# Two edits to a hand-scheduled two-network kernel: other numbers in the emission scheduler's cost table, and the first tile's last normalization released earlier

## The chip, the cores and the metric

The kernel runs on one core of a Trainium2 chip (trn2). The metric is device time in microseconds (us) of one launch, the median of three runs; the profile shows one further execution of the same program. Engines carry the profile's names: PE is the matrix engine (PEld its weight loads), DVE the vector engine, ACT the scalar engine, POOL the third elementwise engine, SP the engine whose queue issues most DMAs.

## The reference, cut to what matters

Two networks of two layers each run one after the other on 256 tokens of width 1024, in float32.

```python
def first_block(x, c, ...):
    sc = jax.nn.silu(c)
    for i in range(DEPTH):
        mod = sc @ w_ada[i] + b_ada[i]
        sh_m, sc_m, g_m, sh_f, sc_f, g_f = jnp.split(mod, 6, axis=-1)
        h = modulate(x, norm_mix[i], sh_m, sc_m)
...
            y = moba_attention(h, w_qkv[j], w_o[j], q_gain[j], k_gain[j])
...
            y = short_conv(h, w_in[j], conv_w[j], w_out[j])
        x = x + g_m[:, None, :] * y
        h = modulate(x, norm_ffn[i], sh_f, sc_f)
        x = x + g_f[:, None, :] * swiglu(h, w_gate_up[i], w_down[i])
    return x
```

The second network has, in layer 2, a gated linear recurrence (`hgrn2_mix`) beside a small attention into 256 memory tokens, in layer 3 a stick-breaking attention beside the same kind of memory attention. After each of them comes `wo`, a layer norm with the residual (`post_norm`), then a mixture of 16 experts (two per token, chosen inside one of four groups) and a last layer norm, `(xf - mu) * rsqrt(var + eps) * g + b`, whose result is the output of the kernel.

## The kernel before, in words

The 256 tokens are two tiles of 128 rows, T0 and T1, which share every weight. Weights arrive as units of 128 x 1024 float32 (512 KB each, one DMA of the SP queue, tile `raw`, issued at L555 in `pump`). For float32 accuracy a dense unit is split into two parts: `hi`, a cast (L506 on ACT, or L502 on DVE), and `lo`, the remainder (a subtraction, L487, on DVE). A block is then three products, hi by hi, hi by lo and lo by hi, all issued at L452 in `mm`. Activations are transposed on PE against the identity `identr` (L464 in `tr`) and split in the same way. So a quarter of a dense product (`gemm`, q0 to q3) is six matmuls with 512 columns on PE, beside one cast and one subtraction of 1024 columns for its next weights.

`Body` holds one Python generator per piece of work: a program for each tile, one that prepares weights (`prep_task`), one for the modulation vectors (`ada_task`), one for the transposed and split inputs of a layer (`lhsT_task`), one for the experts. `Sched.run` steps them one at a time: it picks, among those whose conditions hold at a model time `sch.now`, the one with the highest priority. Every helper issues its instruction at once and then moves a model clock: `mm` and `tr` add to `sch.now`, helpers for ACT and DVE to `tA` and `tD`, `pump` adds to `dma_t` for each unit. On the chip the engines run their instructions in the order in which they were issued, and wait for real semaphores. The model numbers therefore choose an order; they appear nowhere else in the program.

In the feed-forward layers (`ffn`, eleven steps e0 to e10 per tile) a step is four quarters of gate and up, then `Silu` and a product on the gate (ACT L480, DVE L487), two transposes of the hidden tile `tH`, its split, and a down product of twelve matmuls. The next layer's input is made by `modnorm` (a sum of squares on ACT L478, a power on POOL L521, a scaling on DVE L492) and `lhsT_task` (eight transposes, four activations L484 and a cast L506 for each half, a subtraction L487). Between ffn1 and layer 2 there is no norm: T0's and T1's `x` are transposed directly.

The last layer norm is done in two ways. T1 goes through `affine_rows`: four instructions on DVE (L498) and a send after each half. T0 goes through `affine_pool`: a bias `nb` on DVE (L494), two activations on ACT (L484), then for the first half a multiplication and an addition on POOL (L1316), for the second half the same two on DVE (L487). Two events order them: `fin1` is set when T1's statistics have been issued, `sentf1` when T1's four DVE instructions have been. Behind it all, `go` copies a flag that says whether a second, denser version of the experts must run; it does not run on this data.

Of the kernel before, what the change touches and what calls it, by code (L numbers as in the profile page):

```python
# [72 lines left out]
def make_plan(again=False):  # L73
# [75 lines left out]
    for nm, kd in moe(0)[:16] + lnrows("m0") + moe(0)[16:]:  # L149
        put(nm, kd, 1)  # L150
# [4 lines left out]
    for nm, kd in moe(1)[:16] + lnrows("m1") + moe(1)[16:]:  # L155
        put(nm, kd, 1)
# [145 lines left out]
class Body:  # L302
# [148 lines left out]
    def mm(self, out, lhsT, rhs, start, stop, shared=False):  # L451
        self.nc.tensor.matmul(out, lhsT, rhs, start=start, stop=stop, skip_group_check=shared)  # L452
        n = 1
        for d in rhs.shape[1:]:
            n *= d
        m = out.shape[0]
        if lhsT.dtype == F32R:
            c = max(0.227 * n / 512, 0.108)
        else:
            c = max(0.86 * n / 512, 0.224 if m > 64 else 0.112) * (0.26 if m <= 32 and n == 512 else 0.52 if m <= 64 and n == 512 else 1.0)  # L460
        self.sch.now += c

    def tr(self, out, in_):
        self.nc.tensor.transpose(out, in_, self.ident)  # L464
        self.sch.now += 0.109

    def act(self, out, in_, func, bias=0.0, scale=1.0, accum_out=None):
        want = {AF.Exp: "natural_log_exp_and_others", AF.Ln: "natural_log_exp_and_others", AF.Silu: "silu_and_others"}.get(func)
# [68 lines left out]
    def pump(self):  # L537
        while self.can_dma():
            i = self.nextdma
            if i == 4 and not self.again:  # L540
                self.nc.sync.dma_start(self.x[0], self.x_d[0])
                self.dma_t += 1.46
                self.x0_t = self.dma_t + 2.0
            if i == 18 and not self.again:
                self.nc.sync.dma_start(self.x[1], self.x_d[1])
                self.nc.sync.dma_start(self.cst, self.consts_d[:, 128:])
                self.dma_t += 2.3
                self.x1_t = self.dma_t + 2.0
            if self.plan.kind[i] == "row":
                t = self.ring.tile([128, 1024], F32, tag="u", name="row")  # L550
                r = self.rows_d[self.where[self.plan.src[i]]]
                self.nc.sync.dma_start(t, bass.AP(tensor=r.tensor, offset=r.offset, ap=[[0, 128], [1, 1024]]))
            else:
                t = self.ring.tile([128, 1024], F32, tag="u", name="raw")
                self.nc.sync.dma_start(t, self.units_d[self.where[self.plan.src[i]]])  # L555
            self.tiles[i] = t
            self.dma_t = max(self.dma_t, self.sch.now) + 1.3
            self.arr[i] = self.dma_t + 2.0
            if self.plan.kind[i] != "dense":
                self.ready[i] = self.arr[i]  # L560
            self.raw_used += 1
            if self.plan.kind[i] == "dense":
                self.rawdense += 1
            self.nextdma += 1
# [335 lines left out]
    def mem_task(self):  # L900
# [43 lines left out]
        self.fS(4)  # L944

    def mem_attention(self, T, layer, qm, mm):

        hi, lo = [mm[:, i * 256:(i + 1) * 256].rearrange("p (k t) -> p k t", k=2) for i in range(2)]
# [355 lines left out]
    def affine_pool(self, T, nm, src):  # L1304

        x, sv = self.x[T], self.stat[T]
        rows = self.rows(nm)
        yield [self.unit(r) for r in rows]
        nb = self.tm(1)
        self.ts(nb, sv[:, 0:1], sv[:, 2:3], -1.0, ALU.mult, ALU.mult)  # L1310
        for b in range(2):
            c = slice(b * 512, (b + 1) * 512)
            self.act(x[:, c], src[b], AF.Identity, bias=nb, scale=sv[:, 2:3])
        ops = list(zip((ALU.mult, ALU.add), [self.tiles[r] for r in rows]))
        for op, r in ops:
            self.nc.gpsimd.tensor_tensor(x[:, :512], x[:, :512], r[:, :512], op)  # L1316
        self.nc.scalar.dma_start(self.out_d[T][:, :512], x[:, :512])
        yield f"sent{nm}"
        for op, r in ops:
            self.tt(x[:, 512:], x[:, 512:], r[:, 512:], op)  # L1320
        self.send(T, slice(512, 1024))
        for r in rows:
            self.done(r)
# [26 lines left out]
    def wo_postnorm(self, T, layer, mix, mm):  # L1350
        front = not (self.again or self.last[T])

        def res(b):
            def f(acc):
                self.residual_half(T, b, acc)
                if front:
                    self.sch.spawn(self.front_half(T, b, layer), 0)
            return f

        if T == 0:  # L1360
            self.LAG = 8
        tail = [(mm[:, j * 128:(j + 1) * 128], mm[:, 256 + j * 128:384 + j * 128]) for j in range(2)] + [f"memat{layer}_{T}"]
        yield from self.gemm(T, self.ids[f"wo{layer}"], mix, [res(0), res(1)], tail=tail)
        self.fS(2)
        self.fH()
        self.stats(T, self.bns[T])
        if not front:
            yield from self.affine_rows(T, f"m{layer}", self.halves(T))
# [24 lines left out]
    def layer2(self, T):  # L1393
# [71 lines left out]
        def b6(acc):  # L1465
            nonlocal mm
            qm, mm = self.tH(), self.tH(F32R)
            self.scopy(qm[:, :256], acc[:, :256])
            self.free()
            self.sch.spawn(self.mem_attention(T, 0, qm, mm), 0)  # L1470
# [664 lines left out]
    def moe(self, T, layer):  # L2135
        if T == 0:
            self.SMIN = SM0
            self.sel, self.selT, self.xs = {}, {}, {}
            self.sch.spawn(self.moe_task(layer), 2)
        yield from self.moe_front(T, layer)  # L2140
        st = self.tm(12)
        for b in range(2):
            yield f"moe{layer}_{T}_{b}"
            if T == 1 and not self.last[T]:
                yield lambda: self.tD - 0.3
            acc = self.out[T]
            self.nc.vector.bn_stats(st[:, 6 * b:6 * b + 6], acc[b])
            self.onD(512)
        self.stats(T, st)
        if T == 0 and self.last[T]:  # L2150
            yield f"fin{layer}"
            yield from self.affine_pool(T, f"f{layer}", acc)
        else:
            self.sch.set(f"fin{layer}")
            yield from self.affine_rows(T, f"f{layer}", acc)
            self.sch.set(f"sentf{layer}")
        self.free(2)
# [125 lines left out]
```

## Time and profile before

| | us |
|---|---|
| median of three runs | 1204.48 (1203.82, 1204.48, 1207.32) |
| the profiled execution, its own time | 1204.19 |
| its span, first to last instruction | 1202.4 |
| PE busy / idle inside the span | 1144.9 / 57.5 |
| DVE busy, ACT busy, POOL busy | 725.0, 549.1, 44.8 |
| mean granted clock of PE | 0.988 |

The time outside the span is 1.8 us. PE is busy for 95% of the span, so most of what a change of order can move is inside the 57.5 us in which PE stands still (7 us of them at the start, before the first weights have been prepared, and 13 us at the end, behind the last matmul). The list of waits says what PE waited for, the timeline where; the table of windows gives busy time, granted clock and DMA share for each stretch.

### The profile page before, as it was taken

How to read it: one execution, taken by the hardware profiler on the slowest of the kernel's cores; microseconds unless marked ns; L12 is line 12 of the kernel's file. 1: busy time of each engine (PE TensorE's matmuls, PEld its weight loads, DVE VectorE, ACT ScalarE, POOL GpSimd, SP SyncE). 2: the span in 40 equal slices, each digit the busy share in tenths (PEclk: the TensorE clock that was granted, in tenths of full speed). 3: DMA queues.
4: the chain of work that ended last, by engine and by line, in shares of the span. 5: the costliest groups of instructions: out<-in, count | busy, mean ns of one | idle time of the engine just before them, and what ended most of it. 6: DMA issues, size and time to landing. Idle time of an engine off the chain costs nothing. (4 is left out here: it accounts for less than half of the span.)

```text
span 1202.4 us, 16685 instructions
## 1 busy us (share of the span) xinstructions
PE 1144.9 (95%) x6344; PEld 823.7 (69%) x6344; DVE 725.0 (60%) x1121; ACT 549.1 (46%) x913; POOL 44.8 (4%) x65
## 2 busy tenths in 40 slices
PE   7999989999998999999999999999999899999995
PEld 4777768888886787788887789886333577673331
DVE  4577667667577987665556567678221766564214
ACT  4655465434446455544434484553121456631211
POOL 0021000000000000000000000100000100000001
PEclk9999999999999999999999999999999899999998
DMA  9976768777664866466556233377999842587994
GB/s 375 409 306 228 256 222 302 262 268 269 244 239 155 340 247 215 158 211 217 205 194 209 86 125 105 123 277 266 378 409 408 311 142 72 188 333 306 408 408 159
DMA packets 83544, 301.72 MB, mean 251 GB/s; under 512 B 9408, under 2 KB 9824, under 8 KB 83456
## 3 DMA queue, kind: packets, MB, share of 16 engines
q1 hardware_dynamic: 82224, 298.37, 67.1%
q0 software_dynamic: 944, 1.82, 0.6%
q8 instruction: 52, 0.85, 0.3%
q10 hardware_dynamic: 288, 0.38, 0.1%
q14 instruction: 36, 0.29, 0.1%
HBM read 298.83 MB, written 2.10 MB: 250 GB/s over the span
## 5 line engine op out<-in xcount | busy, mean ns | idle before, releaser
L452 PE MATMUL bk<-hi,tS 128*128 128x512 f32 (+1 forms) x1760 | 586.9, 399 | 13.7 <-ACT hi L506 8.0
L452 PEld LDWEIGHTS bk<-hi,tS 128*128 128x128 f32 x1760 | 332.6, 190 | 87.2 <-ACT hi L506 8.7
L487 DVE TENSOR_TENSOR lo<-raw,hi 128x1024 fp32r<-128x1024 f32 x266 | 317.1, 1221 | 67.4 <-ACT hi L506 65.7
L452 PE MATMUL bk<-lo,tS 128*128 128x512 f32 (+1 forms) x880 | 345.0, 392 | 1.6 <-DVE lo L487 1.6
L506 ACT CAST hi<-raw 128x1024 fp32r<-128x1024 f32 x263 | 265.0, 1049 | 20.8 <-DMA raw<-in_units_dram 8.2
L452 PEld LDWEIGHTS bk<-lo,tS 128*128 128x128 f32 x880 | 167.4, 190 | 35.0 <-DVE lo L487 3.4
L480 ACT ACTIVATE tH<-bk 128x256 f32<-128x256 f32 (+1 forms) x100 | 44.8, 449 | 253.8 <-PE bk L452 253.6
L452 PE MATMUL bk<-hi,tH 128*128 128x512 f32 x384 | 133.1, 397 | 1.4 <-ACT tH L506 1.4
L487 DVE TENSOR_TENSOR tH<-tH,bk 128x256 f32<-128x256 f32 x60 | 25.1, 419 | 143.4 <-ACT tH L480 143.3
L452 PE MATMUL bk<-raw,tB 128*32 128x512 f32 x768 | 89.1, 594 | 0.4 <-DVE tB L494 0.4
L452 PEld LDWEIGHTS bk<-hi,tH 128*128 128x128 f32 x384 | 72.3, 189 | 17.1 <-ACT tH L506 2.1
L452 PE MATMUL bk<-raw,tH 128*32 128x512 f32 x640 | 80.1, 594 | 0.6 <-DMA raw<-in_units_dram 0.5
L452 PE MATMUL bk<-lo,tH 128*128 128x512 f32 x192 | 75.1, 391 | 0.0
L498 DVE SCALAR_TENSOR_TENSOR tS<-raw,cs,tS 128x1024 f32<-128x1024 f32 x52 | 66.6, 1280 | 0.3
L452 PEld LDWEIGHTS bk<-raw,tB 128*32 128x32 f32 x768 | 23.2, 110 | 52.4 <-issue 45.9
L498 DVE SCALAR_TENSOR_TENSOR tS<-bk,gsl,tS 128x512 fp32r<-128x512 f32 x32 | 23.3, 749 | 56.2 <-ACT tS L480 55.8
L464 PE MATMUL bk<-identr,tH 128*128 128x128 f32 x296 | 49.9, 277 | 6.8 <-DVE tH L487 3.0
L452 PEld LDWEIGHTS bk<-raw,tH 128*32 128x32 f32 x640 | 22.1, 109 | 49.0 <-issue 39.8
L464 PEld LDWEIGHTS bk<-identr,tH 128*128 128x128 f32 x296 | 36.1, 140 | 28.1 <-issue 8.2
L506 ACT CAST tH<-bk 128x256 fp32r<-128x256 f32 (+1 forms) x52 | 18.5, 356 | 67.5 <-PE bk L464 65.3
L480 ACT ACTIVATE tS<-bk,gsl 128x512 fp32r<-128x512 f32 x32 | 21.1, 686 | 60.7 <-PE bk L452 60.7
L506 ACT COPY tH<-bk 128x256 f32<-128x256 f32 (+1 forms) x56 | 25.6, 474 | 49.0 <-PE bk L452 38.6
(197 smaller groups left out, 990.8 us busy)
## 6 DMA issues: line engine op xcount, KB each, us to landing
raw<-in_units_dram SPq DMA_DIRECT2D x556, 512.0 KB, 5.7
row<-in_rows_dram SPq DMA_DIRECT2D x9, 512.0 KB, 7.6
x<-in_x_dram SPq DMA_DIRECT2D x2, 512.0 KB, 9.6
xsave<-x POOLq DMA_DIRECT2D x2, 512.0 KB, 5.0
out_dram<-x SPq DMA_DIRECT2D x3, 256.0 KB, 2.0
ulv<-in_ulv_dram POOLq DMA_DIRECT2D x1, 384.0 KB, 7.2
cst<-in_consts_dram SPq DMA_DIRECT2D x1, 274.0 KB, 11.2
out_dram<-x ACTq DMA_DIRECT2D x1, 256.0 KB, 2.0
```

What stands on the lines that cost most here:

```text
L452: self.nc.tensor.matmul(out, lhsT, rhs, start=start, stop=stop, skip_group_check=shared)
L464: self.nc.tensor.transpose(out, in_, self.ident)
L480: self.nc.scalar.activation(out, in_, func, scale=scale)
L487: self.nc.vector.tensor_tensor(out, a, b, op)
L498: self.nc.vector.scalar_tensor_tensor(out, a, s, b, op0, op1)
L506: self.nc.scalar.copy(out, a)
```

## The change

The costs with which the scheduler advances its model clock get other numbers: a matmul of 512 columns in the split format counts 0.216 instead of 0.227, a transpose 0.07 instead of 0.109, a DMA unit 1.46 instead of 1.3; those of the plain float32 products change a little. Of the table two lines:

```diff
-            c = max(0.227 * n / 512, 0.108)
+            c = 0.216 * max(n, 512 if n < 256 else n) / 512
...
-            self.dma_t = max(self.dma_t, self.sch.now) + 1.3
+            self.dma_t = max(self.dma_t, self.sch.now) + 1.46
```

In the tail, `moe` no longer makes T0 wait for T1's statistics before `affine_pool`; the wait now stands inside it, behind the bias and the two activations. The multiplication of T0's second half is issued ahead of the wait for T1's four DVE instructions, the addition behind it.

```diff
             self.act(x[:, c], src[b], AF.Identity, bias=nb, scale=sv[:, 2:3])
+        yield f"fin{nm}"
         ops = list(zip((ALU.mult, ALU.add), [self.tiles[r] for r in rows]))
...
         self.nc.scalar.dma_start(self.out_d[T][:, :512], x[:, :512])
-        yield f"sent{nm}"
         for op, r in ops:
             self.tt(x[:, 512:], x[:, 512:], r[:, 512:], op)
+            yield f"sent{nm}"
         self.send(T, slice(512, 1024))
...
         if T == 0 and self.last[T]:
-            yield f"fin{layer}"
             yield from self.affine_pool(T, f"f{layer}", acc)
         else:
-            self.sch.set(f"fin{layer}")
+            self.sch.set(f"finf{layer}")
             yield from self.affine_rows(T, f"f{layer}", acc)
```

Three places in the order of instructions show what this moves. Before on PE, from ffn0 into layer 1 (`tH` is T1's hidden tile at its last step, `tS` behind `identr` T0's normalized input, `tH,ones` the modulation vectors):

```order
L464 MATMUL bk<-identr,tH 128x128 x2
L464 MATMUL bk<-identr,tS 128x128 x8
L452 MATMUL bk<-hi,tH 128x512
L452 MATMUL bk<-lo,tH 128x512
L452 MATMUL bk<-hi,tH 128x512 x2
L452 MATMUL bk<-lo,tH 128x512
L452 MATMUL bk<-hi,tH 128x512
L452 MATMUL bk<-tH,ones 128x512 x2
```

and the same place with the change:

```order
L452 MATMUL bk<-lo,tS 128x512
L452 MATMUL bk<-hi,tS 128x512
L464 MATMUL bk<-identr,tS 128x128 x8
L464 MATMUL bk<-identr,tH 128x128 x2
L452 MATMUL bk<-hi,tS 128x512
L452 MATMUL bk<-lo,tS 128x512
L452 MATMUL bk<-hi,tS 128x512 x2
```

T1's two transposes have moved behind T0's eight, and the down product and the modulation vectors, which stood between those eight and layer 1's first product, no longer stand there: layer 1 (`hi,tS`) follows at once.

Before on PE, from ffn1 into layer 2 (`x_82` is T0's row tile, `x_83` T1's):

```order
L452 MATMUL bk<-hi,tS 128x512 x2
L452 MATMUL bk<-lo,tS 128x512
L452 MATMUL bk<-hi,tS 128x512
L464 MATMUL bk<-identr,x_82 128x128 x8
L464 MATMUL bk<-identr,tH 128x128 x2
L452 MATMUL bk<-hi,tS 128x512
L452 MATMUL bk<-lo,tS 128x512
```

and with the change:

```order
L452 MATMUL bk<-tH,ones 128x512 x2
L464 MATMUL bk<-identr,tH 128x128 x2
L452 MATMUL bk<-tH,ones 128x512 x2
L452 MATMUL bk<-hi,tH 128x512
L452 MATMUL bk<-lo,tH 128x512
L452 MATMUL bk<-hi,tH 128x512 x2
```

followed, after the rest of T1's down product, by

```order
L452 MATMUL bk<-hi,tH 128x512 x2
L452 MATMUL bk<-lo,tH 128x512
L452 MATMUL bk<-hi,tH 128x512
L464 MATMUL bk<-identr,x_82 128x128 x8
L464 MATMUL bk<-identr,x_83 128x128 x8
L452 MATMUL bk<-hi,tS 128x512
```

Both pairs of modulation vectors have moved behind T1's last gate and up product, and T1's eight transposes stand directly behind T0's; before, they came behind six quarters of T0's first products and T1's down product.

Before on DVE, the last instructions (`x_83` is T1, `x_82` T0):

```order
L494 TENSOR_SCALAR tm<-stat_92 128x1
L498 SCALAR_TENSOR_TENSOR tS<-bk,gsl,tS 128x512
L2147 BN_STATS tm<-bk 128x6 x2
L1270 BN_AGGR stat_93<-tm 128x2
L494 TENSOR_SCALAR tm<-stat_93 128x1
L494 TENSOR_SCALAR tm<-stat_92 128x1
L498 SCALAR_TENSOR_TENSOR x_83<-bk,stat_93,row 128x512
L498 SCALAR_TENSOR_TENSOR x_83<-x_83,stat_93,row 128x512
L498 SCALAR_TENSOR_TENSOR x_83<-bk,stat_93,row 128x512
L498 SCALAR_TENSOR_TENSOR x_83<-x_83,stat_93,row 128x512
L487 TENSOR_TENSOR x_82<-x_82,row 128x512 x2
```

and with the change:

```order
L494 TENSOR_SCALAR tm<-stat_92 128x1 x2
L498 SCALAR_TENSOR_TENSOR tS<-bk,gsl,tS 128x512
L2148 BN_STATS tm<-bk 128x6 x2
L1270 BN_AGGR stat_93<-tm 128x2
L494 TENSOR_SCALAR tm<-stat_93 128x1
L487 TENSOR_TENSOR x_82<-x_82,row 128x512
L498 SCALAR_TENSOR_TENSOR x_83<-bk,stat_93,row 128x512
L498 SCALAR_TENSOR_TENSOR x_83<-x_83,stat_93,row 128x512
L498 SCALAR_TENSOR_TENSOR x_83<-bk,stat_93,row 128x512
L498 SCALAR_TENSOR_TENSOR x_83<-x_83,stat_93,row 128x512
L487 TENSOR_TENSOR x_82<-x_82,row 128x512
```

T0's bias has moved ahead of the last instruction that works for the experts, and one of T0's two row products ahead of T1's four instructions.

## Rows read from the trace of the kernel before

**Rows 1.** The page's first part: busy time, share and instructions by engine.

```profile
PE 1144.9 (95%) x6344; PEld 823.7 (69%) x6344; DVE 725.0 (60%) x1121; ACT 549.1 (46%) x913; POOL 44.8 (4%) x65
```

**Rows 2.** Windows: window, its length; busy by engine; PE clock, DMA share, GB/s.

```profile
690.00:830.00 140.00, 135.39 (x820) 117.40 (x819) 96.83 (x179) 79.13 (x150) 6.22 (x8) 1.00 0.52 182
830.00:935.00 105.00, 101.47 (x827) 36.91 (x829) 33.84 (x80) 21.83 (x39) 1.69 (x3) 1.00 0.95 374
```

**Rows 3.** Timeline, PE: start, length, instructions; in brackets idle before, its releaser.

```profile
363.71 0.44 PE L464 MATMUL bk<-identr,tH 128*128 128x128 f32 x2 [0.93 <-DVE tH L487]
366.01 1.06 PE L464 MATMUL bk<-identr,tS 128*128 128x128 f32 x8 [1.86 <-DVE tS L492]
...
370.56 0.39 PE L452 MATMUL bk<-hi,tS 128*128 128x512 f32 x1
```

**Rows 4.** Timeline, DVE, the same stretch, ffn0 into layer 1.

```profile
362.08 1.22 DVE L487 TENSOR_TENSOR lo<-raw,hi 128x1024 fp32r<-128x1024 f32 x1
363.24 0.42 DVE L487 TENSOR_TENSOR tH<-tH,bk 128x256 f32<-128x256 f32 x1
...
366.12 1.27 DVE L498 SCALAR_TENSOR_TENSOR tS<-raw,cs,tS 128x1024 f32<-128x1024 f32 x1
368.08 0.69 DVE L487 TENSOR_TENSOR tH<-tS,tH 128x512 fp32r<-128x512 f32 x1 [0.69 <-ACT tH L506]
```

**Rows 5.** Timeline, ACT, the same stretch.

```profile
362.82 0.38 ACT L480 ACTIVATE tH<-bk 128x256 f32<-128x256 f32 x1 [3.86 <-PE bk L452]
363.10 1.05 ACT L478 ACTIVATE tS<-x 128x1024 f32<-128x1024 f32 x1
...
367.43 0.62 ACT L506 CAST tH<-tS 128x512 fp32r<-128x512 f32 x1 [2.87 <-DVE tS L498]
367.95 1.50 ACT L484 ACTIVATE tS<-bk,mcol 128x128 f32<-128x128 f32 x4
...
372.07 0.58 ACT L506 COPY tS<-bk 128x512 f32<-128x512 f32 x1
```

**Rows 6.** Timeline, PE, ffn1 into layer 2.

```profile
652.03 0.44 PE L464 MATMUL bk<-identr,tH 128*128 128x128 f32 x2 [0.71 <-DVE tH L487]
...
680.20 0.50 PE L452 MATMUL bk<-hi,tS 128*128 128x512 f32 x1 [2.38 <-ACT tS L506]
```

**Rows 7.** Timeline, PE, one step of ffn0.

```profile
289.16 0.50 PE L452 MATMUL bk<-hi,tH 128*128 128x512 f32 x1 [0.46 <-ACT tH L506]
```

**Rows 8.** Timeline, PE, layer 2.

```profile
761.41 1.58 PE L452 MATMUL bk<-tB,tS 128*128 128x128 f32 x12 [2.51 <-DVE tB L487]
...
781.32 0.44 PE L464 MATMUL bk<-identr,tH 128*128 128x128 f32 x2 [0.47 <-ACT tH L506]
```

**Rows 9.** Timeline, PE, the last units of the first experts.

```profile
934.52 1.92 PE L452 MATMUL bk<-raw,tH 128*32 128x512 f32 x16 [0.23 <-DMA raw<-in_units_dram]
```

**Rows 10.** Timeline, DVE, the end.

```profile
1193.59 1.74 DVE L487 TENSOR_TENSOR x<-x,row 128x512 f32<-128x512 f32 x1
```

**Rows 11.** Timeline, POOL, the end.

```profile
1193.19 1.59 POOL L1316 TENSOR_TENSOR x<-x,row 128x512 f32<-128x512 f32 x1
```

**Rows 12.** Timeline, PE, layer 2's first products, a fall of the clock and behind it.

```profile
682.77 1.06 PE L452 MATMUL bk<-hi,tS 128*128 128x512 f32 x2
...
684.05 1.06 PE L452 MATMUL bk<-hi,tS 128*128 128x512 f32 x2
...
686.05 0.61 PE L452 MATMUL bk<-hi,tS 128*128 128x512 f32 x2
...
686.73 0.61 PE L452 MATMUL bk<-hi,tS 128*128 128x512 f32 x2
```

**Rows 13.** Windows at both transitions; columns as in rows 2.

```profile
363.00:368.00 5.00, 2.42 (x15) 2.04 (x16) 3.09 (x6) 2.13 (x6) 0.56 (x1) 1.00 1.00 396
...
680.00:684.00 4.00, 3.80 (x11) 2.81 (x12) 3.83 (x5) 3.47 (x5) 0.00 (x0) 0.74 0.02 4
```

More of the change, by code (lines that the diff above doesn't have):

```diff
@@ L457, in mm @@
         if lhsT.dtype == F32R:
-            c = max(0.227 * n / 512, 0.108)
+            c = 0.216 * max(n, 512 if n < 256 else n) / 512
         else:
-            c = max(0.86 * n / 512, 0.224 if m > 64 else 0.112) * (0.26 if m <= 32 and n == 512 else 0.52 if m <= 64 and n == 512 else 1.0)
+            c = max(0.858 * n / 512, 0.11) * (0.26 if m <= 32 and n == 512 else 0.53 if m <= 64 else 1.0)
         self.sch.now += c
@@ L464, in tr @@
         self.nc.tensor.transpose(out, in_, self.ident)
-        self.sch.now += 0.109
+        self.sch.now += 0.07
     def act(self, out, in_, func, bias=0.0, scale=1.0, accum_out=None):
```

## The prediction

> **What bounds the kernel now.** I read the page's busy times first, then the windows by stage, the list of PE's waits, and the timeline around the longest of them. PE is busy for 95% of the span, DVE for 60%, ACT for 46% [rows 1]. No matmul is added or taken away, so PE's work stays what it is, and what the change can move is idle time of PE, half-clock time of PE, and the end behind the last matmul. Idle time comes in short waits. The windows show it by stage: 140 less 135.4 is 4.6 us in layer 2, where the clock is full and the DMA half used; the first experts (830 to 935) have 3.5 us idle in 105, at a DMA share of 0.95 [rows 2]. The timeline shows whom PE waits for: not memory, but the next small step on DVE or ACT (a product, a scaling, a split), where a stage begins and PE has nothing else in its queue [rows 3, 6, 8].
>
> **The table.** It costs and saves nothing by itself: it chooses an order. But how well an order covers the waits depends on how near its model is to the chip. Three 512-column matmuls of the split format take 0.68 us at the full clock, 686.05 to 686.73, so 0.227 each [rows 12]. That is the old number; the new one, 0.216, is 5% short. An order made with PE too fast expects DVE and ACT to lag more than they do, and puts other things forward. What that does is seen only place by place, where the order differs. A quarter of a dense product is six such matmuls, 1.36 us. All durations below are of one profiled execution, whose own time is 1204.19 us.
>
> *From ffn0 into layer 1.* Before, PE waits 0.93 us for T1's hidden tile and 1.86 for T0's normalized input, then works without a stop from 366.01 to 370.56 [rows 3]. In the new order three waits stand there. (a) T1's transposes at its step e9 come directly behind T0's at e10. In DVE's queue T1's product stands behind T0's product, one instruction of the modulation vectors and a split. From the end of T0's quarter that is Silu 0.38 [rows 5] and 0.42 + 1.27 + 1.22 + 0.42 [rows 4], 3.7 us, against one quarter and two transposes on PE, about 1.55; idle 2.2. (b) T0's sum of squares now stands on ACT behind a modulation copy (0.58) [rows 5]. From its start at 363.10 to the transposes at 366.01 the chain took 2.91 [rows 3, 5]; with some 0.5 of the copy ahead and one quarter (1.36) beside it, idle 2.05. (c) Behind the eight transposes layer 1's first product follows at once, but its input needs four activations (1.50), a cast (0.62) and, for the third product, a subtraction (0.69) [rows 4, 5]. Before, T1's down product and a modulation pair lay beside that; now only two transposes do. From the first transpose 0.45 + 1.50 + 0.62, less 1.05 of transposes, is 1.55, and 0.3 for the subtraction: 1.85. Together 6.1 against 2.8: **+3.3**. Bounds: 0, if DVE and ACT run ahead here, and +5, if no part of the three chains has cover.
>
> *From ffn1 into layer 2.* Before, 0.71 and 2.38 us of idle [rows 6]. The 2.38 go: T1's input is now ready before T0's first four quarters end. In their place: both modulation pairs come behind T1's last quarter. The first takes 1.27 on DVE, 0.62 on ACT, 0.69 on DVE [rows 4, 5], of which I put 0.8 beside that quarter: 1.8. T1's product is queued behind it: 0.45. The second pair: 0.9. T1's eight transposes follow T0's, while on DVE T1's residual (four times 0.69) stands behind T0's; T0's lies beside the twelve down matmuls (2.7), T1's only beside transposes: 1.6. Together 4.75 against 3.1: **+1.7**, with bounds of -2 (first pair covered, and no fall of the clock, which there now is behind the 2.38 [rows 13]) and +4.
>
> *The ffn steps.* In ffn0 three waits of 0.46 us like the one at 289.16 come from a tile's down product standing directly behind its transposes [rows 7]. The new order issues T1's twelve in one go, later; all three go, and I leave 0.3 for a new one: **-1.1** (0 to -1.4).
>
> *Layer 2's mixers.* The order differs most here. T1's recurrence moves forward among T0's, its quarters that before filled the memory attention are used up earlier, and the two tiles' memory attentions stand side by side. The wait of 2.51 on the recurrence's DVE chain has a quarter of T0 moved in front of it; but the hops of the memory attention, of which one showed 0.47 before [rows 8], lose their filler. Below, the whole idle of the stage that such a filler could save is 1.5. Above, four hops at 0.47 and one split made late, 1.05 of cast (ACT's cast has the length of the sum of squares in rows 5) and 1.22, give 4.2. I take **+1.0**, nearer the lower half, because the slower real PE gives DVE and ACT more time than the model thinks.
>
> *At nothing.* Layer 0 into ffn0, layer 1 into ffn1 and layer 3 keep their order at the places with waits. In the experts the new order puts the last hidden transposes ahead of a down product, some 1.5 us of possible wait per layer, but the stage is set by the unit queue: PE waits for the last units [rows 9] at a DMA share of 0.95 [rows 2], so the same time is merely spent earlier. If that cover is gone, it costs 3 in all.
>
> *The tail.* DVE's row product of T0 takes 1.74 where such an instruction of 512 columns takes 0.69 elsewhere [rows 4]. POOL's addition ends at 1193.19 + 1.59 = 1194.78, the product at 1195.33, 0.55 later [rows 10, 11]: it finished behind POOL's instruction, not beside it. The change moves this product ahead of T1's four, away from POOL; the product then delays T1's four by 0.69, POOL starts a little earlier, as ACT's part no longer waits for T1's statistics, and the last addition still ends behind POOL's. I take **-0.4**, with bounds 0 and -0.8. The Trainium skill, page SBUF — State Buffer, section "Who interferes with whom", has it as a rule: a DVE instruction with two SBUF inputs and a GpSimd instruction that reads SBUF exclude one another for a whole instruction. By that rule the tail gains 0.4; were the two free to overlap, it would gain 0.8. The trace agrees with the rule, with its 0.55 behind POOL's end.
>
> **The sum.** 3.3 + 1.7 - 1.1 + 1.0 - 0.4 = +4.5, so 1208.7 in an execution like the one profiled. The median of the runs is 0.3 above that execution: 1209.0, against 1204.48.
>
> **The rivals.**
>
> *The waits only change places.* The new waits replace old ones of equal length, as ffn1 into layer 2 shows in part, and PE at 95% leaves little. For it: the totals are made of waits of 0.3 to 2.5 us whose causes stay. Against it: in both transitions filler is visibly gone. It gives -1.5 for the steps and the tail and half of the other 6.0: 1206.
>
> *Faster.* The point that decides is whether DVE is ahead where T1's product waits. If its modulation work is done before T0's quarter ends, (a) vanishes and (b) shrinks to 1.5, so that ffn0 into layer 1 costs +0.5; the first pair of ffn1 vanishes too, 2.95 stand against 3.1, and the fall of the clock behind the 2.38, worth 1.6, goes: -1.75. Layer 2 loses the 2.51 and gains 1: -1.5. With the steps and the tail, -1.5, that is -4.25: 1200.2. For it: DVE is free 40% of the span [rows 1]. Against it: the modulation instruction and the split stand ahead of T1's product in DVE's queue.
>
> *The clock falls more often.* Behind the 2.38 before 680.20 [rows 6] the granted clock falls: the window 680 to 684 has 0.74, and three matmuls take 1.28 us, 682.77 to 684.05, instead of 0.68 [rows 12, 13]; the eight or so that run that way lose 1.6. That is the lower of the two levels, 1.2 GHz instead of 2.4. (a), (b) and (c) stand within a dozen microseconds, and so do the waits of the memory attention; a fall at each adds 3.2 to my sum: 1212. Against it: 0.93 and 1.86 drew none at the first transition, where the window 363 to 368 has 1.00 [rows 3, 13]. The Trainium skill, page TensorE: Matmul & The Clock Gate, section "A second HAM failure mode: psum-queue depth-cycling", says that frequent short idles alone make the clock swing, and would put this rival ahead of my forecast; the trace bears it out in part, since the waits at one transition drew a fall and those at the other did not.
>
> *The tail does not move.* The order shows that it does; were the product to wait anyway, the sum changes by 0.4.
>
> **How the numbers follow.** My sum has 0.36, the exchange of places 0.30, faster 0.19, the clock 0.15. A measurement of this kernel can tell about 0.3%, 3.6 us, from no change: the borders are 1200.9 and 1208.1. The faster rival lies mostly below the first, the exchange between them, my sum mostly and the clock wholly above. That gives faster 0.19, same 0.33, slower 0.48. For 8 times in 10 the range runs from 1200.5, where the faster rival lies, to 1214, where the clock's falls meet part of the upper bounds. Faster and slower being both possible, my sum's own range is 1206 to 1212.
>
> **What would show it.** At ffn0 into layer 1, three waits for DVE `tH`, DVE `tS` and ACT `tS` of about 2 us each; at ffn1 into layer 2, waits before `tH,ones` and between `x` transposes, and none of 2.38 before T1's first product; no 0.46 in ffn0; four or more short waits in the memory attention; in the tail one row product of 0.69 ahead of T1's four instructions and the flag's copy some 0.4 earlier behind the last matmul. PE's busy time should stay at 1145 unless the clock falls, and its idle grow by 5. Idle that does not grow, or waits that are absent at both transitions, make the forecast wrong.

## The result and the profile after

| | before | after |
|---|---|---|
| median of seven runs on the same chip | 1205.42 (1203.82 to 1207.32) | 1213.23 (1212.14 to 1218.98) |
| the profiled execution, its own time | 1204.19 | 1213.23 |
| its span | 1202.4 | 1211.4 |
| PE idle inside the span, up to its last matmul | 44.3 | 50.3 |

The ratio of after to before is 1.0073, 95% interval 1.0054 to 1.0092: slower by 0.7%, +8.8 us by this ratio and +7.8 by the two medians. PE's idle time is its span less its busy time [rows 1], less the 13.2 us (after: 13.6) behind the last matmul. Here is the page's first part of the changed kernel, in the columns of [rows 1].

```profile
PE 1147.5 (95%) x6344; PEld 826.6 (68%) x6344; DVE 723.8 (60%) x1123; ACT 547.1 (45%) x911; POOL 45.5 (4%) x65
```

The number of matmuls is the same. PE is busy for 2.6 us more, its idle time up to the last matmul is 6.0 more, and behind the last matmul lie 0.4 more: together the 9.0 by which the span of the profiled execution grew. The windows say in which stage the idle time lies. Of the changed kernel, columns as in [rows 2]; idle is the window less PE's busy time:

```profile
0.00:340.00 340.00, 328.94 (x1645) 259.41 (x1646) 226.19 (x302) 172.41 (x279) 23.27 (x35) 1.00 0.77 283
340.00:375.00 35.00, 29.43 (x122) 23.38 (x121) 24.46 (x30) 18.18 (x31) 0.56 (x1) 0.90 0.65 241
375.00:650.00 275.00, 269.68 (x1239) 220.89 (x1238) 184.25 (x250) 135.72 (x206) 3.71 (x6) 0.99 0.62 217
650.00:690.00 40.00, 38.04 (x174) 30.65 (x173) 23.53 (x32) 20.26 (x32) 0.00 (x0) 1.00 0.39 138
690.00:830.00 140.00, 129.94 (x772) 111.54 (x771) 89.89 (x160) 71.10 (x134) 5.66 (x7) 0.98 0.45 156
830.00:1180.00 350.00, 336.83 (x2319) 175.74 (x2318) 162.49 (x330) 124.62 (x223) 8.06 (x12) 0.99 0.79 302
```

| stage | idle before | idle after | change | predicted |
|---|---|---|---|---|
| up to 340: layer 0, ffn0's steps | 12.9 | 11.1 | -1.8 | -1.1 |
| 340 to 375: ffn0 into layer 1 | 3.6 | 5.6 | +2.0 | +3.3 |
| 375 to 650: layer 1, ffn1 | 6.4 | 5.3 | -1.1 | 0 |
| 650 to 690: ffn1 into layer 2 | 3.4 | 2.0 | -1.4 | +1.7 |
| 690 to 830: layer 2's mixers | 4.6 | 10.1 | +5.5 | +1.0 |
| 830 to 1180: experts, layer 3 | 12.7 | 13.2 | +0.5 | 0 |
| from 1180 to the last matmul | 0.7 | 3.1 | +2.4 | 0 |

Up to the end of layer 2 both kernels reach a stage within some 6 us of the same time, so a wait near an edge can change windows. That matters once: 1.3 us of waits behind layer 2, at 824 and 825 before and at 830 and 832 after, left its window; layer 2's own waits grew by 6.6, and the stages behind it have 0.8 less.

**ffn0 into layer 1.** PE's timeline of the changed kernel (start, length, instructions; in brackets the idle before and its releaser) shows the three waits that were forecast, where [rows 3] has two, and the 2.8 us of [rows 3] are 5.6:

```profile
348.97 0.44 PE L464 MATMUL bk<-identr,tH 128*128 128x128 f32 x2 [2.01 <-DVE tH L487]
...
363.28 1.09 PE L464 MATMUL bk<-identr,tS 128*128 128x128 f32 x8 [1.96 <-DVE tS L492]
...
366.19 0.79 PE L452 MATMUL bk<-hi,tS 128*128 128x512 f32 x1 [1.59 <-ACT tS L506]
```

Three waits of 0.46 in ffn0, one of them in [rows 7], are gone. All products of this form (`hi,tH`, 384 of them) together stood at 1.4 us of idle, released by ACT's `tH`; after, they stand at 0.4, released by DVE, and that is the one wait at 812.74 in layer 2, below.

**ffn1 into layer 2.** The same view. The wait of 2.38 [rows 6] has gone, and what came in its place is short:

```profile
661.75 0.44 PE L464 MATMUL bk<-identr,tH 128*128 128x128 f32 x2 [0.46 <-DVE tH L487]
...
662.48 0.51 PE L452 MATMUL bk<-tH,ones 128*128 128x512 f32 x1 [0.29 <-ACT tH L506]
...
663.21 0.50 PE L452 MATMUL bk<-tH,ones 128*128 128x512 f32 x1 [0.22 <-DVE tH L487]
...
667.61 0.63 PE L464 MATMUL bk<-identr,x 128*128 128x128 f32 x4 [0.28 <-DVE x L487]
...
668.94 0.63 PE L464 MATMUL bk<-identr,x 128*128 128x128 f32 x4 [0.70 <-ACT tS L506]
```

**Layer 2.** PE's timeline again. [Rows 8] has waits of 2.51 and 0.47, and one of 0.20 lay ahead of them, 3.2 us in all. Now there are eight, of 9.8 us:

```profile
712.91 0.73 PE L452 MATMUL bk<-ulv,tS 128*128 128x512 f32 x2 [0.99 <-ACT tS L480]
...
765.84 2.90 PE L452 MATMUL bk<-tB,tS 128*128 128x128 f32 x12 [4.60 <-DVE tB L487]
...
783.03 0.38 PE L452 MATMUL bk<-lo,tS 128*128 128x256 f32 x1 [0.52 <-DVE lo L487]
...
786.51 0.44 PE L464 MATMUL bk<-identr,tH 128*128 128x128 f32 x2 [0.46 <-ACT tH L506]
...
790.99 0.44 PE L464 MATMUL bk<-identr,tH 128*128 128x128 f32 x2 [0.52 <-ACT tH L506]
...
804.85 0.63 PE L464 MATMUL bk<-identr,tH 128*128 128x128 f32 x4 [0.65 <-DVE tH L487]
...
807.17 0.66 PE L452 MATMUL bk<-tH,mv 128*64 128x128 f32 x8 [1.69 <-ACT tH L506]
...
812.74 0.50 PE L452 MATMUL bk<-hi,tH 128*128 128x512 f32 x1 [0.39 <-DVE tH L487]
```

Why the longest grew from 2.51 to 4.60 stands in DVE's timeline ahead of it. Before, in the first row, and with the change, in the others:

```profile
758.74 1.68 DVE L514 COPY_PREDICATED tS<-masks,bk 128x384 f32<-128x384 uint8 x2
...
761.12 0.57 DVE L514 COPY_PREDICATED tS<-masks,bk 128x384 f32<-128x384 uint8 x1
761.59 2.35 DVE L487 TENSOR_TENSOR lo<-raw,hi 128x1024 fp32r<-128x1024 f32 x2
763.85 1.00 DVE L514 COPY_PREDICATED tS<-masks,bk 128x384 f32<-128x384 uint8 x1
764.64 0.59 DVE L487 TENSOR_TENSOR tB<-tB,tm 128x384 f32<-128x384 f32 x1
765.15 0.54 DVE L487 TENSOR_TENSOR tB<-tB,tS 128x384 f32<-128x384 f32 x1
```

With the change, two weight splits, 2.35 us, for products that come later, stand between the two masked copies of T1's recurrence. Before, the two copies followed each other directly (one row of 1.68 for both). PE waits for the end of this chain.

**The tail.** The timeline of all engines at the end of the changed kernel, without the weight loads and the sends:

```profile
1193.54 0.55 POOL L521 TENSOR_TENSOR stat<-tm,mhalf 128x1 f32<-128x1 f32 x1 [112.35 <-DVE tm L494]
1194.13 0.21 DVE L494 TENSOR_SCALAR tm<-stat 128x1 f32<-128x1 f32 x1 [0.73 <-POOL stat L521]
1194.44 1.45 ACT L484 ACTIVATE x<-bk,tm,stat 128x512 f32<-128x512 f32 x2 [3.46 <-DVE tm L494]
1195.78 0.69 ACT L480 ACTIVATE tS<-bk,gsl 128x512 fp32r<-128x512 f32 x1
...
1196.52 0.51 PE L452 MATMUL bk<-tS 128*128 128x512 f32 x1 [2.62 <-ACT tS L480]
...
1197.30 0.50 PE L452 MATMUL bk<-tS 128*128 128x512 f32 x1 [0.28 <-DVE tS L498]
...
1198.89 0.68 DVE L487 TENSOR_TENSOR x<-x,row 128x512 f32<-128x512 f32 x1
1199.12 0.86 POOL L521 TENSOR_TENSOR stat<-tm,mhalf 128x1 f32<-128x1 f32 x1 [5.02 <-DVE tm L494]
...
1199.95 2.93 POOL L1317 TENSOR_TENSOR x<-x,row 128x512 f32<-128x512 f32 x2
1200.32 1.43 DVE L498 SCALAR_TENSOR_TENSOR x<-x,stat,row 128x512 f32<-128x512 f32 x1
...
1203.95 0.13 DVE L502 CAST go<-flag 1x1 int32<-1x1 f32 x1
```

Read from the top: T0's bias (L494) waits for POOL's power, then ACT runs T0's two activations (1.45), and only behind them the scaling `tS` of T1's last expert sum (L480). The last matmuls of the kernel wait for that: 2.62 us, where the same scaling released them after 0.22 before. The same place before, on PE and DVE:

```profile
1187.91 0.51 PE L452 MATMUL bk<-tS 128*128 128x512 f32 x1 [0.22 <-ACT tS L480]
...
1188.70 0.50 PE L452 MATMUL bk<-tS 128*128 128x512 f32 x1 [0.28 <-DVE tS L498]
...
1195.97 0.13 DVE L502 CAST go<-flag 1x1 int32<-1x1 f32 x1
```

Up to the flag's copy the tail is in fact shorter: from the start of the last matmul to the copy 1203.95 - 1197.30 = 6.65, before 1195.97 - 1188.70 = 7.27. So the change gains 0.6 where the prediction looked, and loses 2.4 one step ahead of it. (Behind the copy, up to the end of the span, this execution takes 7.5 us and the one before 6.4, which is why the span behind the last matmul is not shorter.)

### The profile page after: what moved, and what is told of

Read it like the earlier page. It is cut to its first block, busy times and chain, and to the rows that moved or that the text cites. A ratio compares the mean times of both kernels' runs of the same rounds, so it can differ in the third digit from the quotient of the medians.

```text
span 1211.4 us, 16661 instructions
## 1 busy us (share of the span) xinstructions
PE 1147.5 (95%) x6344; PEld 826.6 (68%) x6344; DVE 723.8 (60%) x1123; ACT 547.1 (45%) x911; POOL 45.5 (4%) x65
## 5 line engine op out<-in xcount | busy, mean ns | idle before, releaser
L452 PE MATMUL bk<-hi,tS 128*128 128x512 f32 (+1 forms) x1760 | 590.8, 400 | 12.7 <-ACT hi L506 8.2
L506 ACT CAST hi<-raw 128x1024 fp32r<-128x1024 f32 x261 | 262.0, 1049 | 11.2 <-DMA raw<-in_units_dram 10.5
L480 ACT ACTIVATE tH<-bk 128x256 f32<-128x256 f32 (+1 forms) x100 | 44.7, 448 | 237.0 <-PE bk L452 237.0
L487 DVE TENSOR_TENSOR tH<-bk,tH 128x256 fp32r<-128x256 f32 (+1 forms) x52 | 20.6, 400 | 48.4 <-ACT tH L506 48.4
L480 ACT ACTIVATE tS<-bk,gsl 128x512 fp32r<-128x512 f32 x32 | 21.1, 686 | 57.3 <-PE bk L452 57.3
```

The source lines that it names most:

```text
L480: self.nc.scalar.activation(out, in_, func, scale=scale)
L487: self.nc.vector.tensor_tensor(out, a, b, op)
L506: self.nc.scalar.copy(out, a)
```

## The experiments

Two questions were put. Which of the two edits costs the time, and by which instructions? And inside the table: is a place at fault (layer 2), or a number (products, transposes, units)? Each kernel was timed beside the kernel before, on one chip. Times are medians in us.

### The two edits apart

`e1_table_only` has the first diff of the change and not the second: the new table, the old tail. `e2_tail_only` has the second and not the first; PE's order is that of before.

> The new table with the tail of before. Theory: the 8 us lost are two separate losses, some 2.7 in the tail (ACT's two activations of T0 stand ahead of T1's last expert activation) and some 6 in the order. Then this kernel is 5.5 to 6.5 us slower than before (ratio 1.0045 to 1.0055), its wait of PE before the last two matmuls is back to 0.2 us, and the waits 2.0, 2.0, 1.6 at ffn0 into layer 1 and 4.6 in layer 2 stay as in the changed kernel. Rival: all of it is the order, the tail's wait falls into time that is lost anyway; then 8 to 9 us slower.

> The tail edit with the table of before; PE's order is that of before, ACT's differs in one place. Theory: PE waits 2.6 us for the last tS of T1, and the kernel is 2.3 to 2.9 us slower than before (ratio 1.002). Rival, the prediction's term: the tail gains 0.4 (ratio 0.9997).

Measured: the table alone 1211.54 against 1204.87, ratio 1.0054 (1.0038 to 1.0069); the tail alone 1208.15, ratio 1.0022 (1.0013 to 1.0031). The two add up to 1.0076, where the whole change has 1.0073. With the table alone the waits of 2.01, 1.97 and 1.59 stand at ffn0 into layer 1, 4.59 in layer 2, and the last matmuls wait 0.22. With the tail alone, PE's timeline at the end has the wait by itself:

```profile
1190.72 1.58 PE L452 MATMUL bk<-tS 128*128 128x512 f32 x2 [2.61 <-ACT tS L480]
```

So the tail costs 0.22%, 2.7 us (1.6 to 3.7), and the table 0.54%, 6.5 us (4.6 to 8.3).

### The tail: ACT's queue or DVE's

`e6_product_ahead` is the kernel before with only T0's row product moved ahead of T1's four instructions:

```diff
-        yield f"sent{nm}"
         for op, r in ops:
             self.tt(x[:, 512:], x[:, 512:], r[:, 512:], op)
+            yield f"sent{nm}"
```

`e7_acts_behind_T1` is the tail-only kernel, but ACT's two activations wait until T1's last expert sum has been issued; the bias stays early, and T1's statistics are not waited for:

```diff
         self.ts(nb, sv[:, 0:1], sv[:, 2:3], -1.0, ALU.mult, ALU.mult)
+        yield f"moe{nm[1:]}_1_1"
         for b in range(2):
```

> Before, with only T0's row product moved ahead of T1's four DVE instructions; bias and ACT's activations stay behind T1's statistics. The theory on the shared port says: the product needs ACT's second activation, which here ends only 1.5 us after the statistics, so DVE waits for it and T1's four instructions start some 1.7 us later: 0.5 to 1.5 us slower. Rival: DVE's product no longer waits behind POOL and the end comes 0.4 earlier.

> The table of before and the changed tail, but ACT's two activations of T0 are issued behind T1's last expert activation (ACT's order is that of before); bias and activations still ahead of T1's statistics. Theory: the wait of 2.6 goes back to 0.2, ACT's part is done by the time T1's statistics are, and the end comes 0.4 to 1.0 us earlier than before. Rival: the tail's loss comes from elsewhere (the bias on DVE, POOL's order) and this kernel is 2 us slower as well.

Measured: e6 1206.20 against 1204.87, ratio 1.0008 (0.9996 to 1.0019), no difference that can be told; e7 1204.66, ratio 0.9997 (0.9987 to 1.0008), the loss of e2 gone, but the gain of 0.4 to 1.0 us that was expected is too small to be told in the times. In e7 ACT's order at the end is the scaling first, then the two activations, and the wait is 0.22 again:

```profile
1188.35 0.69 ACT L480 ACTIVATE tS<-bk,gsl 128x512 fp32r<-128x512 f32 x1 [2.40 <-PE bk L452]
...
1189.09 0.50 PE L452 MATMUL bk<-tS 128*128 128x512 f32 x1 [0.22 <-ACT tS L480]
...
1189.40 1.45 ACT L484 ACTIVATE x<-bk,tm,stat 128x512 f32<-128x512 f32 x2 [0.37 <-DVE tm L494]
```

One event more and the loss of e2 is gone, with the order on PE, DVE and POOL unchanged, so ACT's queue is its cause. From the last matmul's start to the flag's copy e7 takes 6.68, much as the changed kernel does (6.65). The product moved alone does not pay in the trace, since it has to wait for ACT and holds up T1's four behind it on DVE; from the last matmul to the copy e6 takes 8.18 instead of 7.27:

```profile
1194.92 1.19 DVE L487 TENSOR_TENSOR x<-x,row 128x512 f32<-128x512 f32 x1 [1.57 <-ACT x L484]
```

### The table: layer 2 or the rest

`e9_old_in_layer2` uses the new numbers everywhere but in layer 2's mixers, where the old ones hold; `e10_new_in_layer2` the other way round. Both have the old tail. A flag, switched where T0 enters layer 2 and its experts, chooses the numbers:

```diff
-        self.sch.now += 0.109
+        self.sch.now += 0.07 if self.fresh else 0.109
...
         if T == 0:
             self.hv, self.gs, self.ktil = {}, {}, None
+            self.fresh = False
...
     def moe(self, T, layer):
         if T == 0:
+            self.fresh = True
```

> The new table everywhere but in layer 2 (from T0's entry into layer 2 to its entry into the first experts the old one holds), old tail. Theory: of the 6 us of the table most are lost in layer 2; with the old numbers there the wait of 4.6 and most of the memory attention's waits go: ratio to before 1.000 to 1.002. Rival: the losses are spread, or come with the state in which layer 2 is entered, and the ratio stays at 1.004 or more.

> The old table everywhere but in layer 2, where the new one holds, old tail. Theory: layer 2 alone loses 4 to 6 us: ratio to before 1.003 to 1.005. Rival: it needs the order in which layer 2 is entered, and this kernel is within 0.1% of before.

Measured: e9 1201.21 against 1205.05, ratio 0.9957 (0.9943 to 0.9971), and e10 1215.98, ratio 1.0082 (1.0069 to 1.0096). Both went past what was expected of them, e9 to the faster and e10 to the slower side. The new numbers lose in layer 2 and gain in the rest, although e9 has the three waits of ffn0 into layer 1 (2.01, 1.96, 1.59). e9 was run again, as `e15_old_in_layer2_again`:

> The kernel with the new table everywhere but in layer 2 once more, with the old tail, beside the repaired one on the same chip. Theory: new numbers gain outside layer 2 and lose in it; ratio to before 0.995 to 0.997. Rival: the 0.9957 was a lucky set of five, and it is 0.998 or more.

Measured: 1201.87 against 1205.01, ratio 0.9979 (0.9967 to 0.9990). That lies between what the theory and the rival said, so the first 0.9957 was probably in part luck; it is faster than before in both, by 0.2 to 0.4%. In e10 the wait on the recurrence is 3.09, again with two splits between the masked copies on DVE (2.34, at 768.58), and another stands in PE's timeline that the changed kernel does not have:

```profile
772.74 2.22 PE L453 MATMUL bk<-tB,tS 128*128 128x128 f32 x12 [3.09 <-DVE tB L493]
...
790.91 0.58 PE L453 MATMUL bk<-lo,tS 128*128 128x256 f32 x1 [4.93 <-DVE lo L493]
```

That second one is a wait for a weight split that came too late on DVE. So layer 2 under the new numbers does not have one fixed loss; the order there depends on what was done before.

### The splits in layer 2 held back

`e8_splits_held` is the table-only kernel in which no new weight split may be issued while T1's last level of the recurrence is under way:

```diff
             for l in range(nl):
+                if T == 1 and quad == 1 and l == 2:
+                    self.hold = True
...
                     self.tt(far[:, :, :64], far[:, :, :64], q3[:, :, :64], ALU.mult)
+                    self.hold = False
```

> The kernel of the new table and the old tail, with the preparation of weights held back while T1's recurrence is at its last level, so that two splits (2.35 us on DVE) no longer stand ahead of the chain for which PE waits 4.6 us. Theory: that wait falls to about 2.3, the rest of layer 2 keeps its waits, and the time falls by 2 to 3 us: ratio to before 1.003 to 1.004. Rival: the wait is set by the chain itself and the splits only come later, so the wait stays near 4 or another split becomes late, and the ratio stays at 1.005.

Measured: 1205.88 against 1205.05, ratio 1.0000 (0.9986 to 1.0015), where the table alone had 1.0054. PE's timeline in layer 2:

```profile
767.57 1.58 PE L452 MATMUL bk<-tB,tS 128*128 128x128 f32 x12 [2.54 <-DVE tB L487]
...
798.53 1.16 PE L452 MATMUL bk<-mkT,tH 128*128 128x256 f32 x4 [1.01 <-DVE tH L502]
```

The 4.60 is 2.54, as long as in the kernel before, and DVE has the two masked copies in one row of 1.68 again. The waits of 0.65 and 1.69 in the memory attention have gone too: what the planner does later follows from what it does here. The whole loss of the table comes back, about 6 us, twice what was expected. Of this the wait on the recurrence is 2.1, and all waits in layer 2 together 4.8: four of them, 5.0 us (0.99, 2.54, 0.46, 1.01), where the table alone has eight of 9.8. The twelve matmuls behind the longest wait, too, take 1.58 instead of 2.90. Put into the kernel before, the same hold moves no instruction at all, so it is not a gain by itself.

### One number at a time

`e3_products_only` has only the new costs of the products, `e5_transpose_only` only 0.07 for a transpose, `e4_dma_only` only 1.46 for a unit, all with the old tail. `e12_products_in_layer2` has the new product costs in layer 2 alone, by e9's flag turned round.

```diff
-            c = max(0.227 * n / 512, 0.108)
+            c = 0.216 * max(n, 512 if n < 256 else n) / 512
...
-            c = max(0.86 * n / 512, 0.224 if m > 64 else 0.112) * (0.26 if m <= 32 and n == 512 else 0.52 if m <= 64 and n == 512 else 1.0)
+            c = max(0.858 * n / 512, 0.11) * (0.26 if m <= 32 and n == 512 else 0.53 if m <= 64 else 1.0)
```

```diff
-        self.sch.now += 0.109
+        self.sch.now += 0.07
```

```diff
-            self.dma_t = max(self.dma_t, self.sch.now) + 1.3
+            self.dma_t = max(self.dma_t, self.sch.now) + 1.46
```

> Of the table only the two costs of matmuls are new (0.216 for 0.227, and the plain float32 ones); transposes, DMA units and the tail as before. Theory: the products' cost moves nearly all of the order and carries the loss: ratio 1.004 to 1.006, waits of 2 us at ffn0 into layer 1 and of over 4 in layer 2. Rival: the transposes' or the DMA's entry is what makes the bad places, and this kernel is within 0.2% of before, on either side.

> Of the table only the transpose is new (0.07 for 0.109). Theory: small either way, 0.998 to 1.002, since 296 of 6344 instructions change their cost by 0.04 us. Rival: one early place changes and the orders behind it differ as much as with the whole table, 0.4% or more on either side.

> Of the table only the DMA unit is new (1.46 for 1.3). Theory: the order depends on the products' cost against that of ACT and DVE, and the stages where PE has waits are not bound by units: the ratio to before stays within 0.999 to 1.002. Rival: units that the model takes for late hold the splits back, and this entry costs 3 us or more.

> The old table, but in layer 2 the new costs of the products alone (transposes and DMA old). Theory: it is the products' cost that makes layer 2's order bad: ratio to before 1.005 to 1.010, with one wait of PE for a late split of 3 us or more. Rival: the transposes' or the DMA's cost does it there; ratio 1.002 or less.

| | this | before | ratio |
|---|---|---|---|
| e3, products | 1222.73 | 1205.05 | 1.0139 (1.0124 to 1.0154) |
| e5, transposes | 1211.58 | 1205.60 | 1.0042 (1.0028 to 1.0057) |
| e4, units | 1204.34 | 1205.60 | 0.9989 (0.9980 to 0.9998) |
| e12, products in layer 2 | 1208.20 | 1205.60 | 1.0023 (1.0014 to 1.0032) |

The three do not add up to the 1.0054 of the table; the products alone are worse than all together, and the transposes alone, expected within 0.2%, lose 0.4%. Nor do the products bring layer 2's long wait: e3 and e12 have 2.51 and 2.50 before the recurrence, so that theory has fallen. What e12 loses stands in the memory attention, where five waits of 3.1 us, the longest 1.46, stand for the 0.47 of before. What e3 and e5 have is a wait elsewhere, from layer 1 into ffn1, where the changed kernel has none (5.00 and 5.48). In e5 that wait is about as long as the whole loss. In e3, which loses some 17 us, it is only a part: PE's busy time is 7.3 longer (1152.2), and the rest was not traced. PE's timeline of e5, and the row of DVE that ends the wait:

```profile
465.53 0.39 PE L452 MATMUL bk<-hi,tS 128*128 128x512 f32 x1
471.40 1.94 PE L464 MATMUL bk<-identr,tS 128*128 128x128 f32 x8 [5.48 <-DVE tS L492]
```

```profile
470.50 0.75 DVE L492 TENSOR_SCALAR tS<-x,tm 128x1024 f32<-128x1024 f32 x1 [0.66 <-POOL tm L521]
```

The same transposes before:

```profile
472.90 1.03 PE L464 MATMUL bk<-identr,tS 128*128 128x128 f32 x8
```

T0's scaling is not late in e5: in the kernel before it stands at 471.17. But there PE has dense products from 465.5 to 472.9, and goes from them into the eight transposes without a wait; in e5 nothing is left to do after 465.9. So this is, by the traces, another mechanism than in layer 2: not a chain that was delayed, but its filler used up before. No run repairs it.

### Repairs

`e13_changed_repaired` is the changed kernel with the added lines of e8 and e7. `e11_old_in_layer2_tail` is e9 with e7's tail.

> The changed kernel as it is, table and tail, with two repairs only: no weights are prepared while T1's recurrence is at its last level, and ACT's two activations of T0 stand behind T1's last expert activation. Theory: these two places are the whole of the loss, 1.0000 from the one and 0.9997 from the other: ratio to before 0.998 to 1.001. Rival: there is a further loss, which the two runs with the old tail or the old table hid, and the ratio stays at 1.003 or more.

> The kernel with the new table everywhere but in layer 2, joined with the changed tail in which ACT's two activations stand behind T1's last expert activation. Theory: the two effects add, 0.9957 and 0.9997: ratio to before 0.995 to 0.996, the best of all. Rival: the 0.9957 does not repeat, and the ratio is 0.998 or more.

Measured: e13 1203.65 against 1205.01, ratio 0.9997 (0.9981 to 1.0013); e11 1202.62 against 1205.60, ratio 0.9976 (0.9965 to 0.9987). In e13 these four lines take back what the change lost. e11, and e9 with the old tail, are faster than both the kernel before and the changed one; e11 fell short of the 0.995 to 0.996 that was expected, and the repaired tail adds nothing to e9 that can be told.

## Why the prediction was right or wrong

The direction was right, and the time lies inside the range, at its edge (1213.23 in 1200.5 to 1214; three of the seven runs lie above it). The size was wrong: the sum had +4.5, and +7.8 came by the medians, +8.8 by the ratio (6.5 to 11.1). Two terms of the sum failed by being far too low: layer 2's mixers, put at +1.0, cost 6.6, because two weight splits came to stand ahead of the recurrence's chain and the memory attention lost its filler, and the tail, put at -0.4, cost 2.7, because of what stands behind ACT's two activations. With the 2.6 by which PE's busy time grew, and which the sum left to a rival, that is 11 us too little. That the total is off by only some 4 is luck: elsewhere the sum was 7 us too high, 3.1 at ffn1 into layer 2, where the term had the wrong sign, 1.3 at ffn0 into layer 1 and 2.6 in gains that it did not have.

Nearly every sign that the prediction named came: the three waits of about 2 us, the waits at ffn1, no 0.46 in ffn0, short waits in the memory attention, the early row product. They speak for the direction and not for the size; the wait of 4.60 and ACT's queue, the two dearest places, are not among them. Point by point:

- **ffn0 into layer 1: right.** (a), (b) and (c) were put at 2.2, 2.05 and 1.85, and measured 2.01, 1.96 and 1.59, with the releasers that were named. (In (c), 0.45 + 1.50 + 0.62 less 1.05 is 1.52 and not 1.55, which changes nothing in the 6.1; no row of the prediction shows the 0.45, and the further 0.3 for the subtraction did not come.) Together that is 5.6 against 2.8, +2.8. By its window the stage lost 2.0 instead of 3.3, since a wait of 0.46 in one of ffn0's steps, at 342.95, and one of 0.23, at 373.95, had also stood in that window before.
- **The ffn steps: right, and small.** The three waits of 0.46 went, 1.4 in all, and the 0.3 left for a new one did not come; the rest of the gain up to 340, some 0.9, was not forecast. But seven of them stand in e3 (only the products new) and three in e5, so it is the set of numbers that removes them.
- **ffn1 into layer 2: wrong in sign,** +1.7 forecast, -1.4 measured. The failed step is the cost of the modulation pairs, of which 0.8 was put beside the quarter, and all of it lay there: of 1.8, 0.45 and 0.9 for the first pair, T1's product behind it and the second pair there came 0, 0.46, and 0.29 with 0.22. DVE's modulation instruction started at 657.71, T1's last two quarters ran on PE from 657.94 to 660.66, and the first pair's matmuls behind them did not wait. T1's residual was put at 1.6; the transposes cost 0.28 and 0.70. What the rival "faster" said of this place was right: "the first pair of ffn1 vanishes too".
- **Layer 2's mixers: the term +1.0 was mis-sized,** 6.6 measured. The failed step is "nearer the lower half, because the slower real PE gives DVE and ACT more time than the model thinks": the very wait that was credited with a quarter of filler grew from 2.51 to 4.60, as two splits, 2.35 us, came to stand ahead of its chain on DVE. The upper bound had the right kind of loss for the memory attention, one late split and hops without filler, and 4.2 is also what stands there: 0.52, 0.46, 0.52, 0.65, 1.69 and 0.39, where 0.47 stood before. That the two 4.2 agree is luck: the hops took 3.7 where they were put at 1.9, and the late split 0.5 where it was put at 2.3. The bounds left out that a split can also be early, and in the way, and that the first wait could grow from 0.20 to 0.99.
- **The tail: wrong,** -0.4 forecast, +2.7 measured (e2). The failed step is "POOL starts a little earlier, as ACT's part no longer waits for T1's statistics". ACT's part does start earlier, and stands with its 1.45 ahead of T1's last scaling in ACT's queue; the prediction asked who waits on DVE and POOL, and not what is queued behind the two activations on ACT. Nor did POOL gain: its multiplication is issued behind T1's power, and starts 2.65 after the last matmul's start instead of 2.74. The part from the last matmul to the flag's copy came out near the forecast, -0.6 against -0.4: the product takes 0.68 instead of 1.74, but T1's second instruction beside POOL now takes 1.43 instead of 0.75. So the delay beside POOL moved to another instruction, which agrees with the rule of the Trainium skill that the prediction drew on (page SBUF — State Buffer, section "Who interferes with whom").
- **At nothing.** Layer 1 and ffn1 gained 1.1 that was not forecast; the experts and layer 3 changed by less than 1, so their cover held.
- **The rival on the clock** came true in part. Behind the three waits of ffn0 into layer 1, and behind the 4.60, the granted clock falls to half, the lower level (windows of the changed kernel):

```profile
365.00:372.00 7.00, 5.82 (x14) 4.52 (x15) 4.28 (x6) 6.23 (x12) 0.00 (x0) 0.53 0.23 75
765.00:772.00 7.00, 6.16 (x21) 5.47 (x22) 2.88 (x5) 1.90 (x3) 0.00 (x0) 0.52 0.24 75
```

  In return the fall behind the 2.38 of ffn1 [rows 13] is gone: 650 to 690 has 1.00 instead of 0.96. What is left is the +2.6 of busy time. The mean granted clock is 0.980 to 0.986 in the seven runs of the changed kernel and 0.987 or 0.988 at the median in the kernel before, so it is hardly this execution alone; which waits the loss goes with was not separated. The order at ffn0 into layer 1 has a clock under 1.00 there (0.85 to 0.95 in 340 to 375) in all seven profiles that contain it; of the eight with the two waits of before, 0.93 and 1.86, three have one (0.90 to 0.95).

What stays open: where exactly the new numbers gain outside layer 2. The windows show -1.8, -1.1 and -1.4 up to 690 against +2.0; no experiment separated these. Why the transposes' or the products' cost alone uses up the filler ahead of ffn1, and the whole table does not, is open too. And e10 was not repaired, so how its loss divides between the early and the late splits is only argued.

## What to carry to other kernels

When a piece of side work is released earlier, list what stands behind it in each engine's queue: here 1.45 us of activations that nobody needed yet, together with the wait for their bias, held up the kernel's last matmuls by 2.4 us, and one event between them and the critical scaling took that back. An emission planner whose cost table changes does not shift the time by the size of its errors: the entries act together (1.0139, 1.0042 and 0.9989 alone, 1.0054 together), so it is better to look in the trace for the two things that an order can do wrong: weight preparation that has come to stand ahead of a serial chain (hold it there explicitly), and products that were used up before the chain that they should cover. A wait that already tops its stage is the place to bound widest upwards.

## What was not expected of the hardware

The granted clock differs between executions in which PE's instructions have the same order. Before, 340 to 375 has 1.00. In e6, whose PE order is that of before, the same window has 0.90 and the same PE waits:

```profile
340.00:375.00 35.00, 31.75 (x134) 25.55 (x133) 24.14 (x31) 17.83 (x31) 0.56 (x1) 0.90 0.56 214
```

There the eight transposes behind the wait of 1.86 take 1.94 us at half the clock, and 1.06 in the kernel before [rows 3]. Over the twelve runs of e13 the time goes from 1201.04 to 1209.07; the three above 1208 have a mean granted clock of 0.984 or 0.985, the five up to 1203 one of 0.987 to 0.993. So single runs of one program differ by as much as the whole change, and a fall of the clock in one profile is no proof that the order causes it. The tail showed smaller things: POOL's power took 0.86 beside DVE's row product instead of 0.55, and from the flag's copy to the end of the span it is 6.4 to 7.5 us in the profiled executions of different kernels.
